# Two attention layers on one core: weight loads traced behind the next block's maxima and tied behind the latest transposes; merges in three steps instead of four

## The chip, the cores and the metric

The kernel runs on 1 core of a Trainium2 chip. The metric is the device time of one execution in microseconds; the time of a kernel is the median of its runs.

## What is computed

A trunk of two layers over x (1 x 1024 x 1024, fp32) with its own weights in each:

```python
for i in range(DEPTH):                       # DEPTH = 2: layer A, layer B
    h = mixer_a(x, ...) if i == 0 else mixer_b(x, ...)
    x = layer_norm(DEEPNORM_ALPHA * x + h, ln_g[i], ln_b[i])
    gate = sigmoid(x @ ple_w_gate[i])
    x = x + gate * (p[i] @ ple_w_proj[i])
```

mixer_a is a windowed attention with 16 heads of 64 in three groups of dilation 1, 4 and 16, each with queries, keys and values of its own, merged by the sums of their softmaxes (x @ w_in is 1024 x 10240). mixer_b is a causal window of 128 with 2 key-value heads for 16 query heads and a sink per head. Either output is multiplied by SiLU(z) and by an output matrix.

## The kernel before

**Arithmetic.** Every fp32 operand of a matmul is split into two fp16 parts, high and low, and a product is three matmuls. A *lin tile* (lines 268 to 270) is 128 tokens by 512 columns: 8 slices x 3 = 24 matmuls of 128x512.

**Weights.** They come in blocks of 1024 x 512 (4 bytes each, 2 MB). `Block.load` (L102) issues four DMAs of 512 KB on SP's queue into the tile `wraw`, of which there are two. `Block.maxima` (L108) lets DVE take the largest absolute value of each chunk, and derives a power-of-two scale. `Block.split` writes the high part on ACT (L131) and the low part on DVE (L132), chunk by chunk, into `whl` (or `wo`, `wg`). `weight_steps` (L554) is a generator that puts these steps in the order split of block i, load of block i + 2 (its `wraw` is then free), maxima of block i + 1; each lin tile pulls 1.6 of its steps (`progress`), `next_block` as many as the block still needs.

**Attention.** A tile of queries and keys goes through `rope_out`: rotation on DVE (L344) and POOL (L346, L347), the parts on ACT (L353) and POOL (L354), a copy on DVE (L357), and a transposing DMA on SP (L358) into `qk` (in layer B `bq`, `bk`). A *score unit* has its matmuls at L381, masked maxima on DVE (L385, L387), exp on ACT (L391), the parts on ACT (L395) and on POOL or DVE (L397), and a transposing DMA (L400) into `pT`. A *value unit* (L412 to L414) multiplies pT with the values; in layer A its result goes through ACT (L655) and SP (L664) to scratch memory `scr`, in layer B through DVE (L815, tile `mu`) and SP (L817) to `ob`. A value unit stands two score units behind its own in layer A, three in layer B.

**Merges.** For each token tile and head pair of layer A a generator `merge` (L697) fetches the three groups (L705), weighs them (L710 to L719) on DVE and ACT, sums on POOL and DVE (L724 to L727) and stores `oa` (L728). `merge_step` takes one step of at most two merges at a time.

**Stages.** Startup; layer A (20 blocks: for each of two pairs of heads and each of three groups a block of values and two of queries and keys, then two blocks of z); `mixed`, which fetches rows of attention output and z (L851, L852, tiles `ot`, `og`), splits them on ACT and DVE (L259, L260), transposes them (L831, `ogT`), multiplies by the output blocks and normalizes; `gate` (x @ ple_w_gate, L933 to L945); layer B (one block of keys and values, two of queries, two of z, whose rows are stored at L686); `mixed` and `gate` again.

**Order.** The program is traced in the order in which Python runs; a planner with a timeline of its own then decides in which order each engine gets its instructions, so that all engines' orders move when the trace does. All DMAs named here go through SP's one queue, in SP's order.

## Time and profile before

| | us |
|---|---|
| median of 3 runs | 1745.78 (1745.37 to 1746.15) |
| profiled execution | 1743.35 |
| its span | 1741.6 |
| PE busy | 1598.4 (92%) |
| DVE, ACT, POOL busy | 1162.5 (67%), 837.5 (48%), 707.3 (41%) |
| mean granted clock of PE | 0.973 |

The table's busy times are sums over the span. Stages lie one behind the other in the profiled execution: startup to some 108 us, layer A to 1091, its projection and gate to some 1300, layer B to 1530, its projection and gate to the end. A number in brackets behind a row of the timeline is the time for which the engine was idle ahead of it, and what ended that.

### The profile page before, as it was taken

The page shows a single profiled execution, that of the slowest core. Times are in us where ns is not written, and L with a number is a line of the kernel's source. Part 1 is how long each engine was busy: PE and PEld are TensorE (multiplying, and loading weights), DVE is VectorE, ACT ScalarE, POOL GpSimd, SP SyncE. Part 2 cuts the span into 40 slices and gives each one's busy share as a digit, 9 for nine tenths or more (in the row PEclk, how much of TensorE's full clock was granted, in tenths as well). Part 3 has the DMA queues.
Part 4 walks back from the last instruction along what each step waited for, and adds up shares of the span by engine and source line. Part 5 has one row for each costly group of instructions (what it writes and reads, how often), then busy time and mean ns, then how long its engine had stood idle before and what let it go on. Part 6 is the DMA issues. An engine that isn't in the chain of part 4 may idle for free. (4 is left out here: it accounts for less than half of the span.)

```text
span 1741.6 us, 29174 instructions
## 1 busy us (share of the span) xinstructions
PE 1598.4 (92%) x10579; PEld 882.9 (51%) x10579; DVE 1162.5 (67%) x2845; ACT 837.5 (48%) x1818; POOL 707.3 (41%) x603
## 2 busy tenths in 40 slices
PE   8599899999999889999999989589999898979998
PEld 3245566664555545666545544234465555534444
DVE  2666665765677677567656776787457988667741
ACT  3422755565455445545546553532334668744221
POOL 0303642551554575335326554343324553123441
PEclk9799999999999999999999999799999999989999
DMA  9325775575688778558647896979974798797973
GB/s 362 149 85 139 141 177 124 129 142 110 153 178 193 186 164 176 131 130 162 140 113 152 162 244 208 315 219 254 261 182 107 145 192 178 146 283 214 236 204 109
DMA packets 542785, 309.06 MB, mean 177 GB/s; under 512 B 473008, under 2 KB 494128, under 8 KB 542256
## 3 DMA queue, kind: packets, MB, share of 16 engines
q1 hardware_dynamic: 542640, 307.20, 71.8%
q8 instruction: 83, 1.36, 0.3%
q14 instruction: 62, 0.51, 0.1%
HBM read 135.82 MB, written 54.92 MB: 110 GB/s over the span
## 5 line engine op out<-in xcount | busy, mean ns | idle before, releaser
L268 PE MATMUL lin<-whl,xhl 128*128 128x512 f16 x1280 | 490.9, 384 | 2.4 <-ACT whl L131 1.9
L269 PE MATMUL lin<-whl,xhl 128*128 128x512 f16 x1280 | 489.2, 382 | 0.0
L270 PE MATMUL lin<-whl,xhl 128*128 128x512 f16 x1280 | 488.9, 382 | 0.0
L391 ACT ACTIVATE sm<-sm,st,cs 128x128 f32<-128x128 f32 (+1 forms) x384 | 203.6, 531 | 167.0 <-DVE st L387 138.7
L397 POOL TENSOR_TENSOR phl<-sm,phl 128x1024 f16<-128x1024 f32 (+1 forms) x88 | 161.3, 1833 | 255.7 <-ACT phl L395 249.9
L108 DVE TENSOR_REDUCE wpm<-wraw 128x1 f32<-128x1024 f32 (+1 forms) x132 | 156.6, 1198 | 94.7 <-DMA wraw<-in_wa_dram 46.9
L270 PEld LDWEIGHTS <-xhl 128*128 128x128 f16 x1280 | 149.4, 117 | 128.9 <-issue 5.1
L268 PEld LDWEIGHTS <-xhl 128*128 128x128 f16 x1280 | 149.5, 117 | 122.7 <-issue 6.7
L269 PEld LDWEIGHTS <-xhl 128*128 128x128 f16 x1280 | 150.3, 117 | 117.5 <-issue 4.3
L346 POOL TENSOR_TENSOR t<-t,t 128x256 f32<-128x256 f32 (+1 forms) x120 | 93.0, 775 | 274.6 <-DVE t L344 202.0
L354 POOL TENSOR_TENSOR hl<-t,hl 128x512 f16<-128x512 f32 (+1 forms) x120 | 141.6, 1180 | 101.9 <-ACT hl L353 101.9
L385 DVE CUSTOM_DVE_ANT_0 sm<-s,tab 128x256 f32<-128x256 f32 (+1 forms) x512 | 157.3, 359 | 30.4 <-PE s L381 26.1
L344 DVE TENSOR_TENSOR t<-lin,tab 128x512 f32<-128x512 f32 (+1 forms) x240 | 147.8, 655 | 30.0 <-PE lin L270 30.0
L132 DVE SCALAR_TENSOR_TENSOR whl<-wraw,s,whl 128x1024 f16<-128x1024 f32 (+1 forms) x116 | 160.3, 1426 | 4.1 <-ACT whl L131 4.1
L353 ACT ACTIVATE hl<-t 128x512 f16<-128x512 f32 (+1 forms) x120 | 72.4, 603 | 174.6 <-POOL t L347 155.4
L131 ACT ACTIVATE whl<-wraw,s 128x1024 f16<-128x1024 f32 (+1 forms) x116 | 122.0, 1123 | 25.1 <-DVE s L208 17.8
L270 PE MATMUL lin<-whl,x2T 128*128 128x512 f16 (+1 forms) x320 | 115.0, 359 | 0.0
L268 PE MATMUL lin<-whl,x2T 128*128 128x512 f16 (+1 forms) x320 | 114.9, 359 | 0.0
L269 PE MATMUL lin<-whl,x2T 128*128 128x512 f16 (+1 forms) x320 | 114.7, 359 | 0.0
L395 ACT ACTIVATE phl<-sm 128x1024 f16<-128x1024 f32 (+1 forms) x128 | 110.7, 865 | 2.2
L412 PEld LDWEIGHTS <-pT 128*128 128x128 f16 x800 | 72.3, 98 | 49.3 <-DMA pT<-phl 47.4
L357 DVE COPY hl<-hl 128x512 f16<-128x512 f16 (+1 forms) x104 | 50.6, 487 | 66.4 <-POOL hl L354 66.3
(186 smaller groups left out, 2942.3 us busy)
## 6 DMA issues: line engine op xcount, KB each, us to landing
wraw<-in_wa_dram SPq DMA_DIRECT2D x56, 512.0 KB, 5.5
scr<-st SPq DMA_DIRECT2D x96, 132.0 KB, 2.5
gt<-scr SPq DMA_DIRECT2D x48, 264.0 KB, 3.4
wraw<-in_wav_dram SPq DMA_DIRECT2D x24, 512.0 KB, 5.7
prh<-pro SPq DMA_DIRECT2D x32, 256.0 KB, 2.7
wraw<-in_wg_dram SPq DMA_DIRECT2D x16, 512.0 KB, 7.1
wraw<-in_wb_dram SPq DMA_DIRECT2D x16, 512.0 KB, 4.8
xg<-y SPq DMA_DIRECT2D x16, 512.0 KB, 3.7
```

What stands on the lines that cost most here:

```text
L108: k.nc.vector.tensor_reduce(pm[:, c:c + 1], self.raw[:, c * q:(c + 1) * q], axis=AX.X, op=ALU.max, apply_absolute_value=True)
L131: nc.scalar.activation(hl[:, 0, sl], self.raw[:, sl], AF.Copy, scale=self.s)
L132: nc.vector.scalar_tensor_tensor(hl[:, 1, sl], self.raw[:, sl], self.s, hl[:, 0, sl], op0=ALU.mult, op1=ALU.subtract)
L268: mm(ps, xh(kt), wh, start=(kt == 0), stop=False)
L269: mm(ps, xh(kt), wl, start=False, stop=False)
L270: mm(ps, xl(kt), wh, start=False, stop=(kt == NK - 1))
L344: nc.vector.tensor_mul(tv, pv, tb[:, n, :].unsqueeze(1).to_broadcast([P, 2 * nh, 32]))
L354: nc.gpsimd.tensor_sub(hl[:, :nh, HD:P], rv, hl[:, :nh, 0:HD])
L385: nc.vector.tensor_tensor_reduce(sm[:, h, :nk], ps[:, i, :nk], mask, 1.0, -3e38, ALU.add, ALU.max, mx[:, h:h + 1])
L391: nc.scalar.activation(sm[:, h, :nk], sm[:, h, :nk], AF.Exp, bias=nbias[:, h:h + 1], scale=cs, accum_out=sums[:, h:h + 1])
L395: nc.scalar.activation(hl[:, 0], sm[:, :, :nk], AF.Copy)
L397: eng.tensor_sub(hl[:, 1], sm[:, :, :nk], hl[:, 0])
```

## The change

`weight_steps` now traces the load of block i + 2 behind the maxima of block i + 1. `rope_out` and `transpose_rows` note the transposing DMA that they traced last (`self.last`), and `Block.load` traces its four DMAs within `issue_after` of that instruction: the planner does not issue them before it. In `merge` one `yield` is gone, so that weights, sum and POOL's multiplications are one step.

```diff
--- before.py
+++ after.py
@@ -94,6 +94,13 @@
         self.done = self.released = False
 
     def load(self):
+        if self.k.last is not None:
+            with self.k.tc.issue_after(self.k.last.ins):
+                self.transfers()
+        else:
+            self.transfers()
+
+    def transfers(self):
         k = self.k
         self.n = NK * self.cols
         self.raw = k.raw.tile([P, NK * 512], F32, tag="wraw", name="wraw")
@@ -152,6 +159,7 @@
         self.o_ps = self.ps_o.tile([P, 2, 4, HD], F32, tag="o", name="o")
         self.o_i = 0
         self.uid = 0
+        self.last = None
         self.bufs = 2
         self.pw = self.wg = None
         self.due = []
@@ -355,7 +363,7 @@
             if nk:
                 src, to = (hl[:, a:b, :].rearrange("p h (w c) -> p h w c", w=2) for a, b in ((nq, nh), (nh, nb)))
                 nc.vector.tensor_copy(to, src[:, :, ::-1, :])
-            nc.sync.dma_start(dst, hl[:, :nb, :].rearrange("p b c -> p (b c)"), transpose=True)
+            self.last = nc.sync.dma_start(dst, hl[:, :nb, :].rearrange("p b c -> p (b c)"), transpose=True)
 
         self.ends.append(parts)
 
@@ -559,10 +567,10 @@
         yield from b[0].maxima()
         for i in range(len(b)):
             yield from b[i].split()
+            if i + 1 < len(b):
+                yield from b[i + 1].maxima()
             if i + 2 < len(b):
                 b[i + 2].load()
-            if i + 1 < len(b):
-                yield from b[i + 1].maxima()
 
     def next_block(self):
         b = self.blocks[self.bi]
@@ -710,7 +718,6 @@
         nc.vector.tensor_reduce(M, nb.rearrange("p g a h -> p a h g"), axis=AX.X, op=ALU.min)
         nc.vector.tensor_sub(w, M.unsqueeze(1).to_broadcast([P, 3, 2, 4]), nb)
         nc.scalar.activation(w, w, AF.Exp)
-        yield
         wl = sp.tile([P, 3, 2, 4], F32, tag="mwl", name="mwl")
         nc.vector.tensor_mul(wl, w, sums)
         L = sp.tile([P, 2, 4], F32, tag="mL", name="mL")
@@ -828,7 +835,7 @@
         self.split(src, s, hl[:, 0, :], hl[:, 1, :])
 
         t = self.tp.tile([P, 2, NK, P], F16, tag="T", name=name)
-        nc.sync.dma_start(t.rearrange("p a k c -> p (a k) c"), hl.rearrange("p a c -> p (a c)"), transpose=True)
+        self.last = nc.sync.dma_start(t.rearrange("p a k c -> p (a k) c"), hl.rearrange("p a c -> p (a c)"), transpose=True)
         dst[i] = t
 
     def mixed(self, l, xres, gate_pool):
```

**How the order moves.** Around the first blocks of layer A's second pair of heads (values, then queries and keys) SP had, before (qk is a transposed query-key tile, pT transposed probabilities, gt, oa and scr belong to merges and value units):

```order
L400 DMA_TRANSPOSE pT<-phl 128x16x128
L705 DMA gt<-scr_0_619 128x528
L705 DMA gt<-scr_0_620 128x528
L728 DMA oa_607<-gt 128x2x256
L664 DMA scr_0_618<-st 128x264
L705 DMA gt<-scr_0_618 128x528
L102 DMA wraw<-in_wa_dram 128x1024 x4
L705 DMA gt<-scr_0_619 128x528
L705 DMA gt<-scr_0_620 128x528
L664 DMA scr_0_618<-st 128x264
L358 DMA_TRANSPOSE qk<-hl 128x12x128
L705 DMA gt<-scr_0_618 128x528
```

and now:

```order
L713 DMA gt<-scr_0_618 128x528
L713 DMA gt<-scr_0_619 128x528
L713 DMA gt<-scr_0_620 128x528
L735 DMA oa_606<-gt 128x2x256
L672 DMA scr_0_618<-st 128x264
L713 DMA gt<-scr_0_619 128x528
L713 DMA gt<-scr_0_618 128x528
L713 DMA gt<-scr_0_620 128x528
L672 DMA scr_0_618<-st 128x264
L366 DMA_TRANSPOSE qk<-hl 128x12x128
L735 DMA oa_607<-gt 128x2x256
L713 DMA gt<-scr_0_618 128x528
```

The four loads of the block have gone from here; in the new order the next loads stand 17 rows further on, behind six more qk and four more pT transposes. In the whole of layer A a block's four loads stand in one piece (before, mostly one and three with transposes between them), on average six lin tiles later in PE's order; at the five later blocks of values the loads of two blocks stand close together, with one qk and one or two pT transposes between them.

On DVE the place is the split of block 7 (s_3692 before, s_3687 now). Before:

```order
L132 SCALAR_TENSOR_TENSOR whl<-wraw,s_3692,whl 128x1024
L387 TENSOR_SCALAR st<-mx,ncs_3195 128x4
L132 SCALAR_TENSOR_TENSOR whl<-wraw,s_3692,whl 128x1024 x3
L357 COPY hl<-hl 128x512
L365 SCALAR_TENSOR_TENSOR vl<-lin,vh 128x2x256
L385 ISA sm,mx<-s,tab 128x128
L385 ISA mx 128x1
L385 ISA sm,mx<-s,tab 128x128
L385 ISA mx 128x1
```

now:

```order
L139 SCALAR_TENSOR_TENSOR whl<-wraw,s_3687,whl 128x1024
L395 TENSOR_SCALAR st<-mx,ncs_3195 128x4
L139 SCALAR_TENSOR_TENSOR whl<-wraw,s_3687,whl 128x1024 x3
L115 TENSOR_REDUCE wpm<-wraw 128x1 x2
L365 COPY hl<-hl 128x512
L115 TENSOR_REDUCE wpm<-wraw 128x1
L373 SCALAR_TENSOR_TENSOR vl<-lin,vh 128x2x256
L393 ISA sm,mx<-s,tab 128x128
L393 ISA mx 128x1
```

The maxima (L108, now L115) that stand behind the split are those of the next block, two at once and a third behind a copy; before, a rotation's copy, a value part and the score maxima (shown as ISA) came first. On PE value units stand later: in layer A ten of the 96 by 0.8 to 1.4 lin tiles, the others less or not; in layer B by 1 tile at the beginning, rising to 3.9 for the last ones. Behind the last value unit of layer B 111 lin matmuls stood before the first one that reads `ogT`; now there are 17.

On SP, ahead of layer B's output projection (t is the row's ot, zb a store of z, y the residual rows), before:

```order
L686 DMA zb_13520<-zu 128x512
L851 DMA ot<-ob_13511 128x1024
L102 DMA wraw<-in_wg_dram 128x1024 x3
L686 DMA zb_13521<-zu 128x512
L102 DMA wraw<-in_wg_dram 128x1024
L852 DMA og<-zb_13519 128x1024
L831 DMA_TRANSPOSE ogT<-rhl 128x16x128 x2
```

now:

```order
L858 DMA ot<-ob_13511 128x1024
L859 DMA og<-zb_13519 128x1024
L838 DMA_TRANSPOSE ogT<-rhl 128x16x128
L873 DMA y<-x_0_12910 128x1024
L858 DMA ot<-ob_13512 128x1024
L838 DMA_TRANSPOSE ogT<-rhl 128x16x128
L109 DMA wraw<-in_wg_dram 128x1024 x4
```

The four loads (`in_wg`) have moved from ahead of the first two ogT transposes to behind them. Ahead of layer A's projection the loads move in the same way, behind the first ogT; the last step of the last merge stands one z tile later in DVE's order.

## Rows read from the trace of the kernel before

**Rows 1.** The page, part 1: busy time of each engine, its share of the span, instructions.

```profile
PE 1598.4 (92%) x10579; PEld 882.9 (51%) x10579; DVE 1162.5 (67%) x2845; ACT 837.5 (48%) x1818; POOL 707.3 (41%) x603
```

**Rows 2.** The waits of PE from 180 to 1090 us (layer A): engine, operation, line, what it waited for; us in total, times, longest.

```profile
PE o L412 <- DMA pT<-phl: 32.3, 22, 3.6
PE s L381 <- DMA qk<-hl: 5.5, 2, 5.2
```

**Rows 3.** PE's timeline, lin matmuls without a stop, the first and the last of 35: start, us, operation.

```profile
604.69 0.38 PE L269 MATMUL lin<-whl,xhl 128*128 128x512 f16 x1
...
612.03 0.38 PE L270 MATMUL lin<-whl,xhl 128*128 128x512 f16 x1
```

**Rows 4.** PE's timeline in layer A, single instructions at the end of a gap; in brackets the idle time before them and what ended it. All are the first matmul of a value unit, except the third, which is that of a score unit. The first two rows are the first and the last of four such stops, the fourth and the fifth the first and the last of ten, the sixth and the seventh the first and the last of three (the prediction says of which kind).

```profile
212.29 0.20 PE L412 MATMUL o<-vh,pT 128*128 128x64 f16 x1 [3.38 <-DMA pT<-phl]
...
1021.65 0.20 PE L412 MATMUL o<-vh,pT 128*128 128x64 f16 x1 [3.57 <-DMA pT<-phl]
...
617.64 0.50 PE L381 MATMUL s<-qk 128*128 128x128 f16 x3 [5.23 <-DMA qk<-hl]
...
351.81 0.20 PE L412 MATMUL o<-vh,pT 128*128 128x64 f16 x1 [0.30 <-DMA pT<-phl]
...
964.87 0.20 PE L412 MATMUL o<-vh,pT 128*128 128x64 f16 x1 [1.46 <-DMA pT<-phl]
...
264.07 0.20 PE L412 MATMUL o<-vh,pT 128*128 128x64 f16 x1 [1.15 <-DMA pT<-phl]
...
725.45 0.20 PE L412 MATMUL o<-vh,pT 128*128 128x64 f16 x1 [0.94 <-DMA pT<-phl]
```

**Rows 5.** SP's timeline around the score unit of the third row of Rows 4: when a DMA was issued, how long the issue took.

```profile
604.79 1.87 SPq L102 DMA_DIRECT2D wraw<-in_wa_dram  x4
...
611.76 1.98 SPq L358 DMA_TRANSPOSE qk<-hl  x1
```

**Rows 6.** The qk tiles, 605 to 620 us: time from issue to landing.

```profile
DMA to landing us min/median/max: 3.7/4.7/5.8
```

**Rows 7.** DVE's timeline, same place.

```profile
609.15 1.22 DVE L108 TENSOR_REDUCE wpm<-wraw 128x1 f32<-128x1024 f32 x1 [0.25 <-DMA wraw<-in_wa_dram]
...
610.98 0.76 DVE L357 COPY hl<-hl 128x512 f16<-128x512 f16 x1
```

**Rows 8.** Windows: stretch, its length, busy time (and instructions) of PE, PEld, DVE, ACT, POOL, the granted clock, the DMA share, GB/s.

```profile
213.00:217.00 4.00, 4.00 (x17) 1.55 (x14) 1.21 (x6) 3.60 (x11) 1.97 (x3) 0.57 1.07 232
616.00:623.00 7.00, 5.36 (x19) 2.50 (x20) 6.39 (x18) 0.74 (x2) 3.90 (x5) 0.51 0.72 169
1022.00:1026.00 4.00, 4.00 (x28) 1.74 (x25) 3.94 (x11) 1.71 (x4) 3.21 (x3) 0.57 0.87 232
```

**Rows 9.** SP's timeline, two transposes of layer A.

```profile
206.05 3.00 SPq L400 DMA_TRANSPOSE pT<-phl  x1
...
1014.42 5.18 SPq L400 DMA_TRANSPOSE pT<-phl  x1
```

**Rows 10.** The waits of SP's queue in layer A (180 to 1090 us).

```profile
SPq L400 <- POOL hl L354: 71.9, 22, 5.5
SPq L400 <- POOL phl L397: 70.0, 19, 6.2
```

**Rows 11.** The waits of DVE in layer A (180 to 1090 us).

```profile
DVE wpm L108 <- DMA wraw<-in_wa_dram: 42.8, 19, 6.2
...
DVE mwl L715 <- ACT mw L712: 5.0, 8, 2.6
```

**Rows 12.** Line 132 on DVE (the low part of the split), 330 to 470 us: count, min/median/max ns, first and last start, forms.

```profile
L132 DVE SCALAR_TENSOR_TENSOR whl<-wraw,s,whl x12: 1271/1278/2180, 335.9 to 434.7; 128x1024 f16<-128x1024 f32 x12
```

**Rows 13.** PE's timeline, the first matmul of layer A's output projection.

```profile
1112.31 0.58 PE L268 MATMUL lin<-whl,ogT 128*128 128x512 f16 x1 [20.94 <-DVE whl L132]
```

**Rows 14.** SP's timeline ahead of layer A's output projection.

```profile
1094.77 0.90 SPq L102 DMA_DIRECT2D wraw<-in_wg_dram  x2
...
1105.09 4.95 SPq L831 DMA_TRANSPOSE ogT<-rhl  x1
```

**Rows 15.** The last value unit of layer B on PE (count, ns, first and last start).

```profile
L412 PE MATMUL o<-bvh,pT x8: 193/193/202, 1529.3 to 1529.9; 128*128 128x64 f16 x8
```

**Rows 16.** DVE's timeline behind the last value unit of layer B.

```profile
1533.73 1.22 DVE L108 TENSOR_REDUCE wpm<-wraw 128x1 f32<-128x1024 f32 x1 [5.95 <-DMA wraw<-in_wg_dram]
```

**Rows 17.** SP's timeline ahead of layer B's output projection.

```profile
1552.28 1.34 SPq L102 DMA_DIRECT2D wraw<-in_wg_dram  x3
...
1557.93 6.09 SPq L831 DMA_TRANSPOSE ogT<-rhl  x1
```

**Rows 18.** PE's timeline, the first matmul of layer B's output projection.

```profile
1566.09 0.61 PE L268 MATMUL lin<-whl,ogT 128*128 128x512 f16 x1 [12.04 <-DMA ogT<-rhl]
```

**Rows 19.** The waits of PE from 1300 to 1530 us (layer B).

```profile
PE o L412 <- DVE mu L815: 17.7, 10, 3.9
PE o L412 <- DMA pT<-phl: 4.1, 4, 1.7
PE s L381 <- DMA bq<-hl: 1.5, 1, 1.5
```

**Rows 20.** Line 102 (loads), the stretch and the columns of Rows 12.

```profile
L102 SPq DMA_DIRECT2D wraw<-in_wa_dram x8: 327/423/433, 342.3 to 437.6; - x8
```

**Rows 21.** The waits of PE over the whole program: the one for weights once the blocks run.

```profile
PE lin L268 <- ACT whl L131: 1.9, 1, 1.9
```

## The prediction

> **What bounds the kernel now.** I read the page first: PE is busy for 1598.4 us of the 1741.6 us span [rows 1], so no other engine bounds the whole, and what a change of order can win is PE's stops. The waits of PE, asked for stage by stage, tell who ends them. In layer A (180 to 1090 us) value units wait 32.3 us in 22 stops for the transposed probabilities pT, and score units 5.5 us for qk [rows 2]. The lin tiles around them run without a stop, 34 steps in 7.34 us, so 0.216 us a matmul and 5.2 us a tile of 24 [rows 3]. A value unit that stood one tile later in PE's order, or whose transpose landed a few us sooner, would not stop.
>
> The timeline of SP tells why they land late. I sort the stops by what SP issued ahead of the transpose. The score unit (5.23 us) and **four** value units (the largest stops with a load, 10.9 us together) follow chunks of a weight load by a few us; **ten** small ones (10.1 us together) have a load a little further ahead; **three** (4.5 us together) lie at a block of values, where there are no qk transposes [rows 4]. The remaining five pT stops (6.8 us) have no load near. The rows of the score unit show that a load delays twice. On SP, four chunks were issued from 604.79, the qk transpose at 611.76, and its issue alone took 1.98 us [rows 5]; it landed after 5.8 us where the quickest of that stretch took 3.7 [rows 6]. On DVE a maximum ran at 609.15, as soon as its chunk was there, ahead of the copy at 610.98 that the transpose needed [rows 7]. After such stops the granted clock falls to the 1.2 GHz level: 0.57 over 213 to 217, 0.51 over 616 to 623, 0.57 over 1022 to 1026 [rows 8]; the four us at 0.57 lose 1.7, the 5.36 busy us at 0.51 lose 2.6. Two pT transposes at the first and the last of these places needed 3.00 and 5.18 us for the issue alone [rows 9].
>
> Against this reading stands SP's own list of waits: it holds transposes back mostly for POOL's subtractions, 71.9 and 70.0 us for the two largest entries [rows 10]. Many transposes are late because vector engines are.
>
> **The change, part by part.** The sum is made against the profiled execution, 1743.35 us, which lies 2.43 us under the median of 1745.78.
>
> *Loads behind the maxima and tied.* Bytes, maxima and splits stay the same in number. In the new order a block's four chunks stand together on SP, behind a transpose, some six lin tiles later than before. DVE loses waits for chunks (42.8 us in layer A for the largest source [rows 11]). I cost that at nothing by itself: it is idle time of an engine off the path, covered by PE's lin tiles, and if that cover were gone it would show as a late pT. What is queued behind the moved maxima matters more: DVE now does the split and up to four maxima in a row, 4 x 1.28 + 4 x 1.22 = 10 us [rows 7, 12], and behind them stand the copies of L357 and the score maxima of L385, on which ACT's exp, POOL's subtraction and SP's transposes wait. Value units stand about a tile (0.8 to 1.4) later in PE's order at these places, which pays for half of the 10 us; the maxima, 4.9 of it, stood near there before too.
>
> Layer A, stop by stop:
> - The score unit: no load stands around its transpose any more. The maximum's 1.22, the 2.1 of late landing (5.8 less 3.7) and half of the lost clock (1.3) go: **-4.5**. Bounds 0 and -7.8 (stop and clock).
> - The four: at the first, the 6.2 us from issue (206.05 [rows 9]) to the unit's start (212.29) shrink to 3.7, so 2.5 of its 3.38 go. The same share of 10.9 is 8; of the two clock dips of 1.7 I count 2.5: **-10.5**. Bounds -3 and -14.3.
> - The ten: the loads leave some and come to stand ahead of others; half, **-5**. Bounds 0 and -10.
> - The three at blocks of values: two blocks, eight chunks, now stand a few rows apart there. **0**; bounds -4.5 and +4 (one more stop like the first of the four).
> - The five without a load: **0**; bounds -4 and +4, inside their own 6.8.
>
> Together -20.
>
> *Layer A to its projection.* PE stops for 20.94 us, until 1112.31 [rows 13], at the end of a chain whose last link is the ogT transpose: issued at 1105.09, 4.95 us in its issue, behind chunks issued from 1094.77 on [rows 14]. The new order has the first ogT ahead of these chunks. With the quickest landing, 3.7 us, PE would start 3.5 us sooner; the last step of the last merge stands a z tile's work later on DVE, for which I take 1.5 off: **-2**. Bounds -5 and +4.
>
> *Layer B to its projection.* Here the change takes cover away. Between the last value unit (1529.3 [rows 15]) and the first matmul that reads ogT stood 111 lin matmuls, now 17: 94 x 0.216 = 20.3 us less. Against that the chain from the unit to ogT gets shorter. A maximum that waited 5.95 us for its chunk ahead of the unit's normalization [rows 16] is gone from there. The transpose issued at 1557.93, 6.09 us in its issue behind chunks of 1552.28 [rows 17], let PE start at 1566.09 [rows 18]; now it stands ahead of the chunks, and with 3.7 us to landing PE starts 4.4 us sooner. Net 20.3 - 5.95 - 4.4 = +10. What it buys: value units stand 1 to 3.9 tiles later in PE's order, so 5 to 20 us more slack for the 23.3 us of stops inside layer B [rows 19] and one clock dip of 1.7. I take half of these 25, -12.5, since 17.7 us of the stops end at DVE's normalization, which an order of PE doesn't quicken: **-2.5**. Bounds +10 (nothing regained) and -15.
>
> *Merges in three steps.* The instructions are the same; a merge ends one step earlier. DVE's multiplication now follows ACT's exp in one step: it waited 5.0 us in 8 places before [rows 11], so at most some 5 us more idle time on DVE, under lin tiles. **0**; bounds -1 and +2.
>
> Sum: -20 - 2 - 2.5 = -24.5, so 1718.85 profiled and **1721.3** as a median.
>
> **The rivals.**
> 1. *The loads only move.* A load behind one transpose stands ahead of the next. For it: eight chunks at blocks of values. Against it: most large stops lie where the new order has no load. Only -4.5 of the score unit and -2.5 of the four stay, the rest is 0: -7, a median of 1738.8. Chance 0.14.
> 2. *Layer B's cover is not regained.* For it: DVE ends most stops there. -20 - 2 + 10 = -12: 1733.8. Chance 0.10.
> 3. *Both.* -7 - 2 + 10 = +1: 1746.8, no change. Chance 0.12.
> 4. *Slower: the vector engines set the transposes.* The place is the 10 us of split and maxima on DVE with the score maxima behind them. For it: SP's waits for POOL [rows 10]. A queue that is free earlier wins only 3 us in A, and the end of layer B still costs 10: +7, a median of 1752.8. It decides where A, B and the passage between them regain less than 10 us together. Chance 0.13.
> 5. *Slower: weights come late.* Blocks were loaded from 342.3 on and split some 90 us later, until 434.7 [rows 12, 20]; loaded at about 385, some 46 us are left, where landing (5.8), maxima (4.9) and the scale take under 20. Before, one stop on weights is known, 1.9 us [rows 21]. If each of 20 later blocks gave one, 38 us would stand against the forecast's gain: 1759.3. Chance 0.03.
>
> The Trainium skill ("DMA: Bandwidth & Descriptors", section "Rules for kernel authors") says to issue a DMA early and to wait for its semaphore late; this change does the reverse, and by that rule the fifth rival would be the likeliest. No run here shows the rule's cost yet: the trace has 46 us to spare.
>
> **How the numbers follow.** The forecast's own chance is 0.48. Rivals 1 and 2 are faster too: 0.48 + 0.14 + 0.10 = 0.72. Within 0.2% (3.5 us, about what a measurement of this kernel can tell from no change) is rival 3, 0.12. Slower: 0.13 + 0.03 = 0.16. The low end goes half of the way from each term to its lower bound, -30, -3.5 and -9: 1703. The high end, 1750, takes in rivals 1 to 3. Left out are rivals 4 and 5 (0.16) and some 0.04 below.
>
> **What would show it.** Right: no stop over 2 us where the score unit stopped, and full clock there; 10 to 18 us of pT stops in layer A where there were 32.3; DVE's waits for chunks there under 15 us; mu stops in layer B near 9 us; some 22 us of stop ahead of layer B's projection. Wrong: pT stops in A of 25 us or more with SP held by POOL as before (rival 4), large stops at blocks of values (rival 1), layer B's stops as they were (rival 2), lin tiles that wait for whl (rival 5).

## The result: 1.2% slower, and the profile after

The changed kernel takes 1764.05 us (median of 4 runs, 1761.18 to 1772.46), the kernel before 1745.57 (4 runs, 1742.90 to 1746.15): ratio 1.0117, 95% interval 1.0081 to 1.0153. The forecast was 1721.3 (1703 to 1750), so sign and range are wrong. The profiled execution took 1761.18 us (span 1759.4). Part 1 of its page answers to [rows 1]:

```profile
PE 1599.0 (91%) x10579; PEld 883.5 (50%) x10579; DVE 1158.3 (66%) x2845; ACT 836.1 (48%) x1818; POOL 705.6 (40%) x603
```

PE is busy for as long as before, to 0.6 us. So nearly all of the 17.8 us by which the span grew are stops, and the question is where. Lin matmuls come in the same sequence in both traces; the start of the same one, after minus before, makes a ledger. Its differences from mark to mark are what a stage lost (+) or won (-). The last two columns give the same figure for the runs below, from one profiled execution of each: those that load the blocks of the stage as before (5 or 6 runs), and those that load them as the change does (7 to 9); a run whose own edit touches the stage in another way is left out.

| stage | until (us, before) | forecast | measured | shift at its end | other runs, as before | other runs, as changed |
|---|---|---|---|---|---|---|
| startup | 114.7 | 0 | -1.2 | -1.2 | | |
| layer A | 1069.9 | -20 | -2.0 | -3.2 | -0.8 to +5.7 | -3.5 to +5.6 |
| A to its projection | 1135.4 | -2 | +6.5 | +3.3 | -2.4 to +0.7 | +4.7 to +6.5 |
| A's projection, gate | 1290.3 | 0 | +2.6 | +5.9 | -1.5 to +1.4 | +2.9 to +7.4 |
| B, and to its projection | 1589.2 | -2.5 | +2.5 | +8.4 | -4.5 to -0.7 | +3.7 to +7.9 |
| B's projection, gate | 1734.2 | 0 | +9.4 | +17.8 | 0.0 to +4.1 | -0.5 to +9.5 |

A few us of one execution say little: the first run below is as quick as before, yet its kept execution (1752.27 us, the slowest of its ten) moves between -1.4 and +5.6 within layer A. Read so, layer A won little if anything. The way from A to its projection, A's projection, and B with the way to its projection cost time in every run that has the change there. In the last stage the two ranges overlap. Waits of PE from 180 to 1090 us, as [rows 2]:

```profile
PE o L420 <- DMA pT<-phl: 29.7, 20, 3.9
PE s L389 <- DMA qk<-hl: 7.4, 1, 7.4
```

pT's stops fell by 2.6 us, where 14 to 22 were forecast, and the score unit's stop grew from 5.23. The same value units, one by one, in both traces (us of stops for pT, in the prediction's groups):

| value units | before | forecast | now |
|---|---|---|---|
| the four | 10.9 | -8 | 5.0 |
| the ten | 10.1 | -5 | 1.7 |
| the three at blocks of values | 4.5 | 0 | 6.9 |
| the five without a load | 6.8 | 0 | 4.3 |
| eight that did not stop for pT before | | no term | 11.9 |

The stops that were to go did go, and others came. Say that a transpose has a load in flight when one of the four chunks was issued ahead of it and has not landed when it is issued. By the issue and landing times of the traces that was so for 25 of the 96 pT transposes of layer A before (5.50 us to landing on average, the others 3.92) and for 14 now (6.45, the others 4.00). The stops behind those with a load in flight fell from 24.1 to 14.7 us; the stops behind the others rose from 8.2 to 15.0. The clock gave nothing either: PE runs at the 1.2 GHz level in four stretches of layer A, as before (now 548 to 551, 610 to 620, 1005 to 1009 and 1036 to 1039 us, at 0.50 each; before, those of [rows 8] and 551 to 555).

PE's timeline, the places of [rows 4] (first row of the four, the score unit) and, between them, a block of values:

```profile
216.92 0.20 PE L420 MATMUL o<-vh,pT 128*128 128x64 f16 x1 [1.47 <-DMA pT<-phl]
...
268.99 0.20 PE L420 MATMUL o<-vh,pT 128*128 128x64 f16 x1 [2.44 <-DMA pT<-phl]
...
614.10 0.50 PE L389 MATMUL s<-qk 128*128 128x128 f16 x3 [7.38 <-DMA qk<-hl]
```

At the first the stop shrank from 3.38 to 1.47, and the granted clock of 213 to 217 is 1.00 where it was 0.57 [rows 8]. It still stops, because the load of a block now stands here. SP's timeline:

```profile
203.97 2.28 SPq L109 DMA_DIRECT2D wraw<-in_wa_dram  x4
206.36 7.11 SPq L408 DMA_TRANSPOSE pT<-phl  x1
```

Tied behind one transpose, the four chunks stand directly ahead of the next. Its issue took 7.11 us where it took 3.00 [rows 9]. At the value block another took 7.79, behind seven chunks of two blocks, and the stop grew from 1.15 to 2.44.

At the score unit no load is near. SP issued the transpose late, and it landed 3.8 us later, as quick as any:

```profile
610.25 1.43 SPq L366 DMA_TRANSPOSE qk<-hl  x1
```

POOL and then DVE show why (timelines):

```profile
602.89 1.04 POOL L729 TENSOR_TENSOR gt<-gt,mw 128x512 f32<-128x512 f32 x1 [0.79 <-DVE mw L726]
603.90 1.04 POOL L730 TENSOR_TENSOR gt<-gt,mw 128x512 f32<-128x512 f32 x1
604.90 1.60 POOL L362 TENSOR_TENSOR hl<-t,hl 128x512 f16<-128x512 f32 x1
```

```profile
606.83 0.93 DVE L722 TENSOR_TENSOR mwl<-mw,gt 128x24 f32<-128x24 f32 x1 [0.29 <-ACT mw L720]
607.80 0.18 DVE L724 TENSOR_REDUCE mL<-mwl 128x8 f32<-128x24 f32 x1
607.90 1.28 DVE L352 TENSOR_TENSOR t<-lin,tab 128x512 f32<-128x512 f32 x2
609.09 0.19 DVE L725 RECIPROCAL mL<-mL 128x8 f32<-128x8 f32 x1
609.32 0.70 DVE L726 TENSOR_TENSOR mw<-mw,mL 128x24 f32<-128x24 f32 x1
609.94 0.28 DVE L365 COPY hl<-hl 128x512 f16<-128x512 f16 x1
```

Steps of a merge (L722 to L730) stand ahead of the subtraction of L362 and of the copy of L365 that the transpose reads.

**A to its projection.** PE's first matmul there, as [rows 13]; then ACT and DVE ahead of it:

```profile
1115.48 0.58 PE L276 MATMUL lin<-whl,ogT 128*128 128x512 f16 x1 [27.32 <-DVE rhl L268]
```

```profile
1101.67 4.25 ACT L138 ACTIVATE whl<-wraw,s 128x1024 f16<-128x1024 f32 x4
...
1105.83 1.13 ACT L267 ACTIVATE rhl<-og,rs 128x1024 f16<-128x1024 f32 x1
```

```profile
1102.84 6.90 DVE L139 SCALAR_TENSOR_TENSOR whl<-wraw,s,whl 128x1024 f16<-128x1024 f32 x4
1109.66 1.27 DVE L268 SCALAR_TENSOR_TENSOR rhl<-og,rs,rhl 128x1024 f16<-128x1024 f32 x1
```

The split of the first gate block now stands ahead of the split of the first row: 4.2 us on ACT, 6.8 on DVE. Before, the row went first:

```profile
1102.22 1.15 ACT L259 ACTIVATE rhl<-og,rs 128x1024 f16<-128x1024 f32 x1 [0.80 <-DVE rs L208]
...
1103.47 1.59 DVE L260 SCALAR_TENSOR_TENSOR rhl<-og,rs,rhl 128x1024 f16<-128x1024 f32 x1 [0.61 <-issue]
```

PE's release by name, "DVE rhl", ended at 1110.93; what it waited for was the transpose behind it, issued at 1110.96.

**A's projection.** A new stop, at a small matmul for the scale of the keys/values block (SP, DVE, PE):

```profile
1168.10 2.24 SPq L109 DMA_DIRECT2D wraw<-in_wbkv_dram  x4
```

```profile
1172.47 0.69 DVE L115 TENSOR_REDUCE wpm<-wraw 128x1 f32<-128x512 f32 x1 [0.77 <-DMA wraw<-in_wbkv_dram]
```

```profile
1183.36 0.26 PE L241 MATMUL s<-mdd,ones 128*128 128x128 bf16 x1 [8.61 <-DVE ri L215]
```

A block is late for PE although no lin matmul waits for its weights: the scale stands in PE's order ahead of the next rows' tiles. (What the matmul reads is `mdd`, which DVE finished at 1183.32.) The late load is one part of it. The last maximum ended at 1176.26, and the four small steps from there to `mdd` took DVE another 7.1 us, because splits and sums of rows stand between them.

**B and its projection.** PE's waits from 1300 to 1545 us, as [rows 19]; the last value unit, as [rows 15] (its time last); the first projection matmul, as [rows 18]:

```profile
PE o L420 <- DVE mu L822: 12.1, 6, 4.3
PE s L389 <- DVE mx L393: 3.6, 2, 2.9
```

```profile
L420 PE MATMUL o<-bvh,pT x8: 192/193/193, 1549.4 to 1550.0; 128*128 128x64 f16 x8
```

```profile
1575.92 0.61 PE L276 MATMUL lin<-whl,ogT 128*128 128x512 f16 x1 [22.17 <-DMA ogT<-rhl]
```

From the last unit to this matmul it takes 26.5 us where it took 36.8, yet the stop grew from 12.04 to 22.17, since the lin tiles that covered it have gone ahead.

**Last projection.** One late row, before and now, then SP's wait of 1626 to 1646 us and the window 1640 to 1656 (columns of [rows 8]):

```profile
1632.49 0.39 PE L268 MATMUL lin<-whl,ogT 128*128 128x512 f16 x1 [1.20 <-DMA ogT<-rhl]
```

```profile
1648.55 0.61 PE L276 MATMUL lin<-whl,ogT 128*128 128x512 f16 x1 [7.27 <-DMA ogT<-rhl]
```

```profile
SPq L873 <- ACT ot L864: 7.3, 1, 7.3
```

```profile
1640.00:1656.00 16.00, 8.73 (x29) 3.27 (x28) 13.47 (x23) 4.64 (x5) 4.72 (x4) 0.68 1.04 256
```

With the stop came the lower level of the clock: 8.73 busy us at 0.68 lose 2.8. Stop (6.1 more than the 1.20 at the same matmul before) and clock make up 8.9 of the +9.4.

### The profile page after: what moved, and what is told of

The parts are those of the page before. It is cut to its first block, busy times and chain, and to the rows that moved or that the text cites. A ratio compares the mean times of both kernels' runs of the same rounds, so it can differ in the third digit from the quotient of the medians.

```text
span 1759.4 us, 29156 instructions
## 1 busy us (share of the span) xinstructions
PE 1599.0 (91%) x10579; PEld 883.5 (50%) x10579; DVE 1158.3 (66%) x2845; ACT 836.1 (48%) x1818; POOL 705.6 (40%) x603
## 4 chain that ended last, share of the span: by engine, by line
PE 42%; DVE 17%; issue 11%; DMA 11%; POOL 10%; ACT 6%; SPq 2%; POOLq 0%; DVEq 0%; ACTq 0%
PE lin L276 12%; PE lin L278 12%; PE lin L277 12%; DVE wpm L115 3%; POOL hl L362 2%; ACT sm L399 2%; DVE whl L139 2%; POOL phl L405 2%; DMA pT<-phl 2%; DMA gt<-scr 2%; DVE sm L393 2%; PE s L389 1%; POOL t L354 1%; PE lin L489 1%; DVE t L352 1%
## 5 line engine op out<-in xcount | busy, mean ns | idle before, releaser
L362 POOL TENSOR_TENSOR hl<-t,hl 128x512 f16<-128x512 f32 (+1 forms) x120 | 146.5, 1220 | 115.2 <-ACT hl L361 115.2
L115 DVE TENSOR_REDUCE wpm<-wraw 128x1 f32<-128x1024 f32 (+1 forms) x132 | 155.4, 1193 | 55.8 <-DMA wraw<-in_wa_dram 17.4
L139 DVE SCALAR_TENSOR_TENSOR whl<-wraw,s,whl 128x1024 f16<-128x1024 f32 (+1 forms) x116 | 167.3, 1484 | 4.1 <-ACT whl L138 4.0
L365 DVE COPY hl<-hl 128x512 f16<-128x512 f16 (+1 forms) x104 | 49.0, 471 | 96.0 <-POOL hl L362 95.7
L276 PE MATMUL lin<-whl,ogT 128*128 128x512 f16 x128 | 52.1, 407 | 56.8 <-DMA ogT<-rhl 29.4
```

What stands on the lines that cost most here:

```text
L115: k.nc.vector.tensor_reduce(pm[:, c:c + 1], self.raw[:, c * q:(c + 1) * q], axis=AX.X, op=ALU.max, apply_absolute_value=True)
L139: nc.vector.scalar_tensor_tensor(hl[:, 1, sl], self.raw[:, sl], self.s, hl[:, 0, sl], op0=ALU.mult, op1=ALU.subtract)
L276: mm(ps, xh(kt), wh, start=(kt == 0), stop=False)
L362: nc.gpsimd.tensor_sub(hl[:, :nh, HD:P], rv, hl[:, :nh, 0:HD])
```

## The experiments

Ratios are to the kernel before, run on the same chip, with the 95% interval. "Shift" is the ledger's number, from one execution.

### Which edit

Each edit of the change alone, then load and tie together:

```diff
# merges only (e1_merge): only the yield is gone
# maxima only (e2_swap): untied, merges in four steps
+            if i + 1 < len(b):
+                yield from b[i + 1].maxima()
             if i + 2 < len(b):
                 b[i + 2].load()
-            if i + 1 < len(b):
-                yield from b[i + 1].maxima()
# tie only (e3_tie): load() as in the change, ahead of the maxima
# both (e4_swap_tie): the change with the yield back
```

> Only the merge in three steps; loads as before. Theory (the time is lost where a layer passes into its projection, and in the projections, because swap and tie together reorder those stages): as before, 1745 within 4 us, since PE's order in layer B and behind it is the one of before. Rival (the shorter merge puts DVE and POOL work ahead of the copies that qk transposes wait for, as at the 7.4 us score stop near 607 of the changed kernel): most of the 18 us, 1755 or more.

1746.52 us, 1.0017 [0.9998, 1.0037]: no difference shown.

> Only the load traced behind the next block's maxima, not tied, merges in four steps. Theory (swap and tie together reorder the passages): as before, 1745 within 4 us; PE's order in layer B is that of before. Rival (late tracing alone makes weights and maxima late): 1755 or more, with larger waits of DVE for chunks.

1745.37, 1.0017 [0.9999, 1.0034]: none either.

> Only the tie behind the latest transpose, loads traced at the old place, merges in four steps. Theory (both together are needed): between 1740 and 1752, since layer B's value units stand only 0.2 tiles later on average and the cover behind the last one is 4.3 tiles where the changed kernel has 0.7. Rival (the tie alone costs the time): 1758 or more, with a stop near 22 us ahead of layer B's projection.

1749.16, 1.0039 [1.0023, 1.0055]. The tie by itself costs 17.0 us of layer A (shift at its end). PE's waits of 180 to 1100 us:

```profile
PE o L420 <- DMA pT<-phl: 46.0, 28, 4.9
PE s L389 <- DMA qk<-hl: 4.3, 2, 4.1
```

Some 9 us came back later, in B and the passages. 23 of the 96 pT transposes have a load in flight and take 7.30 us to landing, where 25 took 5.50 before.

> Swap and tie, merges in four steps. Theory (merges play no part): 1758 to 1768, as the changed kernel, with the stops of some 22 us ahead of layer B's projection and of 27 us ahead of layer A's. Rival (the merges cost the time): 1750 or less.

1759.94, 1.0104 [1.0072, 1.0135]; shift -3.6 at A's end, +11.0 in A's projection (1185.3), +15.0 behind B. Load and tie together make the loss; the merges add nothing that the intervals can tell. The score unit stops for 8.0 us here, with four steps, so its longer stop does not come from the missing `yield` either.

### Which blocks

Blocks 0 to 19 are layer A's, 20 and 21 its projection's, 22 and 23 the gate's, 24 B's keys/values, 25 to 30 B's others, 31 and 32 the last gate's. In the first three runs only the blocks named are loaded as in the change, with merges in four steps; in the last two all but those named.

```diff
+            late = i + 2 <= 19      # p_le19; 22 to 24: p_22_24; 25 to 30: p_25_30; not 20 to 24: q_not20_24; not 25 to 30: q_not25_30
+            if i + 2 < len(b) and not late:
+                b[i + 2].transfers()
             if i + 1 < len(b):
                 yield from b[i + 1].maxima()
-            if i + 2 < len(b):
+            if i + 2 < len(b) and late:
                 b[i + 2].load()
```

> Swap and tie for the blocks of layer A alone, merges in four steps. Theory (each stage answers to the order of its own loads): layer A gains 2 to 4 us up to its last lin tile, as in the changed kernel, and everything behind it stays as before: 1738 to 1746. Rival (the projection stages pay for what layer A does): a stop ahead of A's projection of 26 us or more, 1750 or more.

1745.04, 1.0011 [0.9989, 1.0032]: no difference shown for layer A's twenty blocks, on which -20 was forecast.

> Swap and tie for the blocks loaded during layer B alone (queries, z, its output blocks). Theory: the stops inside layer B fall by 10 to 12 us, and the passage to its projection costs 13 to 18 us, since the last value unit stands 3.9 tiles later and the cover behind it is 0.7 tile: net 2 to 7 us, 1745 to 1752. Rival (the cover is paid back in full by B): 1743 or less.

1750.52, 1.0046 [1.0027, 1.0066]. Shift -10.5 within B and +20.9 from its end to its projection, +10.4 net: the cover that the prediction saw go, and not enough regained. The stop there, 25.55 us, ends at a block's scale (`PE s L241 <- DVE mdd L234`) and not at the row, so cover is not the whole of it in this run.

> Swap and tie for three blocks alone, those loaded while layer A passes into its projection and gate (two gate blocks, the block of keys and values). Theory: the stop ahead of A's projection grows by some 6 us to 27, and a stop for a block's scale (the small matmul on mdd) appears in the projection, 2 to 8 us: 1750 to 1758. Rival (these blocks don't matter): 1745 within 3 us.

1746.69, 1.0014 [0.9994, 1.0034], below the 1750 to 1758 expected. The stop at the scale came (9.18 us). The one ahead of A's projection did not grow (18.59; 27 expected): these three blocks alone do not make it.

> The changed kernel with the old order and no tie for the five blocks 20 to 24 (layer A's output blocks, its gate blocks, the block of keys and values). Theory (their late loads cost the passage to A's projection and the stop for a block's scale inside it): the stop ahead of A's projection is back at 21 us, the stop of 8.6 us for the scale of the keys-and-values block is gone, together 8 to 12 us: 1752 to 1756. Rival (these stops come from merges and rows): 1760 or more.

1757.16, 1.0087 [1.0060, 1.0113]. A's passage stops for 22.59 us, the scale stop is gone; the time is a little above what was expected.

> The changed kernel with the old order and no tie for blocks 25 to 30, those loaded during layer B. Theory (B's order loses more cover behind the last value unit than its stops give back): value units of B stand as before, the stop ahead of B's projection is back near 12 us, and the kernel gains 3 to 10 us: 1754 to 1761. Rival (B as changed is a gain): 1765 or more.

1749.23, 1.0034 [1.0012, 1.0055]. The largest part, some 15 us less than the change, and quicker than expected (1754 to 1761). PE ahead of B's projection:

```profile
1570.34 0.61 PE L276 MATMUL lin<-whl,ogT 128*128 128x512 f16 x1 [7.43 <-DMA ogT<-rhl]
```

The parts do not add: B's blocks cost some 8 us put late alone, and some 15 when everything else is late already.

### What holds the transposes in layer A

```diff
# x_noload: the kernel before without the loads of blocks 2 to 19
+        if 2 <= i <= 19:
+            self.raw = k.blocks[i % 2].raw
+            return
# x_nomax: the change, maxima of these blocks over 1/16 of a chunk
+            w = q // 16 if 2 <= k.blocks.index(self) <= 19 else q
# x_nomerge: the change, merges of the first pair without arithmetic
+        if pair == 0:
+            yield
+            nc.sync.dma_start(...)   # gt, group 0, stored as it is
+            return
# m_before, m_after: no merge steps traced around the score stop
+        if self.hold:
+            return
```

> The kernel before without the weight loads of blocks 2 to 19: they take their raw weights from the tiles of blocks 0 and 1 (values of layer A are thus of other weights); every maximum and split stays. Theory (in layer A most stops come from the vector engines' order, not from loads in SP's queue): value units still wait 15 us or more for pT in layer A, the score stop near 610 stays above 4 us, the gain is under 20 us. Rival (the recorded one: loads in the queue make transposes late): pT stops in layer A under 10 us, the score stop under 2, a gain of 30 us or more.

1740.86, 0.9987 [0.9969, 1.0005]. PE's waits in layer A:

```profile
PE o L416 <- DMA pT<-phl: 15.8, 11, 2.8
PE s L385 <- DMA qk<-hl: 6.0, 3, 4.2
```

No difference is shown in the time. Without any load half of pT's stops stay, and the score unit still stops for 4.23 us. The sum over A's 96 pT transposes from issue to landing is 388.4 us; before 415.5, with the change 418.3, with the tie alone 461.3. All of the loads delay them by 27 us, and the change left that as it was. The 96 qk transposes are another matter: 392.0 without loads, 427.6 before, 407.3 with the change, 404.5 with the tie alone. In layer A `self.last` is always a qk transpose, so the tie clears the way of these, and PE seldom waits for them. (The run lost 13.3 us between 130 and 150 us, where lin tiles waited for splits, and won 14.1 from 180 us to A's end, so with no load at all some 14 us of layer A were there to win, by this one execution.)

> The changed kernel with the maxima of blocks 2 to 19 taken over a sixteenth of each chunk (a block's scale is thus that of fewer weights): DVE's burst of maxima behind a split is 0.4 us instead of 4.9. Theory (in layer A the vector engines' order sets the transposes, the burst being part of it): pT stops in layer A fall from 30 to 20 us or less, the score stop near 607 stays, 10 to 15 us less than the changed kernel. Rival (the queue sets them): 1760 or more.

1754.99, 1.0066 [1.0044, 1.0089]; pT's stops 31.4 us. One unit has 8.05 of them, at 1031 us, where it had 3.87; the others fell from 25.8 to 23.4. So the burst of maxima on DVE (rival 4) sets little of them. The score stop fell to 5.04, and the shift at A's end is -7.4 against -3.2. The time lies between what theory (10 to 15 us less than the change) and rival (1760 or more) expected.

> The kernel before with no merge step taken from the fifth tile of the second pair's first block of values until the third tile of its first block of queries and keys (the steps come later); loads as before, with the four chunks at their place. Theory (the score stop near 612 is the chain of the block's first qk tile, held up by merge steps on POOL and DVE): the stop falls from 5.2 to under 3 us, the half clock behind it may go, 1736 to 1743. Rival (the recorded one, the four chunks ahead of the transpose): the stop stays at 5 us, 1745.

> The changed kernel with the same pause of the merge steps. Theory: the score stop near 607 falls from 7.4 to under 4 us, with 4 to 7 us less than the changed kernel, 1757 to 1761. Rival: the stop stays above 6 us.

1745.71, 1.0015 [0.9995, 1.0034], and 1764.47, 1.0124 [1.0092, 1.0155]; score stops 5.05 and 7.44. The merge's instructions stayed where they were on DVE and POOL, so these two tell nothing.

> The changed kernel with the merges of the first pair of heads left out but for their loads and their store (that half of layer A's output is one group's alone): no merge step on DVE, ACT and POOL around 607. Theory (the first qk tile behind a block of values waits for merge steps on DVE and POOL): the score stop falls from 7.4 to under 4 us, stops of value units between 560 and 600 get smaller, 1757 to 1761. Rival (the chain of that tile is longer than the two lin tiles that cover it, whatever else the engines do): the stop stays above 5 us.

1749.17, 1.0038 [1.0017, 1.0058], quicker than the 1757 to 1761 expected. PE's waits in A, where no qk is left:

```profile
PE o L420 <- DMA pT<-phl: 21.3, 16, 3.1
PE o L420 <- ACT st L663: 6.6, 3, 5.0
PE o L420 <- ACT vh L372: 1.2, 1, 1.2
```

The merges hold the qk transpose of that place; that is shown. Without them A gains 10.6 us over the change (shift -13.8 against -3.2).

### The passages

```diff
# x_tiesplit: the change, the split of block 22 traced behind that of the first row
+                if k.blocks.index(self) == 22:
+                    for i in k.row:
+                        es.enter_context(k.tc.issue_after(i.ins))
# x_y5: the change, the sixth row's residual load behind the seventh ogT
+                with self.tc.issue_after(self.og[6].ins):
+                    nc.sync.dma_start(y, xres(n))
# x_xg3: x_y5, and the fourth row's store too
+                with self.tc.issue_after(self.og[6].ins):
+                    nc.sync.dma_start(xg_dr[n], y)
# x_fix3: x_tiesplit and x_xg3, and block 24 loaded as before
+            late = i + 2 != 24
```

> The changed kernel with one more tie: the split of the first gate block (whl) stays behind the split of the first row of attention output on ACT and DVE; nothing else in those two orders moves there. Theory (the longer stop ahead of layer A's projection comes from that split, 4.25 us on ACT and 6.9 us on DVE ahead of the row): PE's first matmul on ogT starts 4 to 7 us sooner, the stop is 20 to 23 us instead of 27.3, 1755 to 1761. Rival (the late loads or the transpose's landing set it): the stop stays above 25 us, 1762 or more.

1756.53, 1.0090 [1.0059, 1.0121]. The stop fell to what was expected, and the passage lost 0.9 us where the change lost 6.5. In the whole time the interval overlaps that of the change (1.0081 to 1.0153), so the gain is shown at this place only:

```profile
1109.39 0.59 PE L281 MATMUL lin<-whl,ogT 128*128 128x512 f16 x1 [22.14 <-ACT ot L871]
```

> The changed kernel with one load moved: that of the sixth residual row of the last projection stays behind the transpose of the seventh row of attention output. Theory (SP stands for 7.3 us with that load, until a row tile comes free, with a transpose behind it that PE needs): the stop of 7.3 us near 1641 is gone and the last stages cost 6 to 9 us less: 1754 to 1760. Rival (the transpose is late for its own row's sake): the stop stays above 5 us, 1762 or more.

1763.86, 1.0123 [1.0089, 1.0156]; the stop is 6.57 us. SP is held at the next thing in its order:

```profile
SPq L898 <- POOL y L897: 9.8, 2, 7.9
```

> The changed kernel with two DMAs of the last projection moved behind the transpose of the seventh row of attention output: the sixth residual load and the store of the fourth normalized row, on which SP stood for 7.9 us when the load alone was moved. Theory (SP is held by whichever of them is issued ahead of that transpose): the stop near 1641 falls from 7.3 to under 2 us, 6 to 9 us less than the changed kernel: 1754 to 1760. Rival (the row itself is late): the stop stays above 5 us, 1762 or more.

1764.57, 1.0118 [1.0093, 1.0143]; 6.72 us, SP held 8.1 us at the store of the row before that. With both DMAs moved SP stands at a third, so these two runs alone don't acquit it. The changed kernel's trace does; DVE, the low part of the seventh row:

```profile
1641.25 1.27 DVE L268 SCALAR_TENSOR_TENSOR rhl<-og,rs,rhl 128x1024 f16<-128x1024 f32 x1
```

It ended at 1642.52. SP was free from 1640.59; it issued another row's transpose (1641.39, 2.59 us) and this one's at 1644.08. SP delays the row by 1.6 us at most: the row itself is late, and that theory falls. What makes it late stays open.

> The changed kernel with three edits at once: the first gate block's split behind the first row's, the keys-and-values block loaded in the old order and untied, and the two DMAs of the last projection moved. Theory (the time over the kernel before is three stops of the projections, each of its own): the stop ahead of A's projection 22 us, no stop for the keys-and-values block's scale, none over 2 us near 1641, together 14 to 20 us less than the changed kernel: 1744 to 1750, no faster than the kernel before. Rival (what is removed at one stop returns at the next): 1755 or more.

1758.85, 1.0080 [1.0052, 1.0109]; 1744 to 1750 was expected. The passage keeps 21.7 us, the scale stop is gone, but the rows behind it stop now, and 6.9 us are lost there from 1185.3 to 1226.9. PE's waits of 1085 to 1300 us:

```profile
PE lin L281 <- ACT ot L877: 21.7, 1, 21.7
PE lin L281 <- DMA ogT<-rhl: 5.0, 4, 3.4
PE lin L281 <- DVE y L898: 3.7, 3, 2.9
PE lin L281 <- DVE p2t L211: 2.0, 1, 2.0
```

Some of a stop that is taken away comes back at the next. No version beat the kernel before.

## Why the prediction was wrong, point by point

- **Layer A, -20 (measured -2.0): the step that failed most.** Not the terms that were to shrink: the four and the ten lost 14.3 us of stops, where 13 were forecast. What failed are the terms at 0 beside them. "No load stands around its transpose any more" was read from the places that had stopped. Eight other units stop now, for 11.9 us, and the three at blocks of values grew by 2.4. Part of it is the first rival (0.14): a load tied behind one transpose stands ahead of the next. Fewer pT transposes have a load in flight (14 for 25), but each takes longer (6.45 us for 5.50), and the sum from issue to landing stays (415.5 and 418.3 us). The larger part is not: only 2.8 of the 11.9 us lie at transposes with a load in flight, the stops without one rose from 8.2 to 15.0, and with no load at all 15.8 us of stops stay. So some 16 us of the 32.3 were never the loads' to give. What sets the new ones stays open; two of the eight (183 and 194 us, 3.2 us together) stand 0.7 and 1.2 lin tiles earlier in PE's order than before. At the rows at 203.97 and 206.36 the chunks landed from 209.8 to 213.7 us and the transpose issued behind them at 216.9. The Trainium skill ("DMA: Bandwidth & Descriptors", section "Two DMAs through the same engine are not ordered") says that within one queue of one DMA engine descriptors start in order, and these landings agree.
- **Score unit, -4.5.** The load ahead of it was real but not the last cause: without loads 4.23 of 5.23 us stay. In the changed kernel merge steps on POOL and DVE are: the stop goes without merges. Neither "no stop over 2 us" nor "full clock" came true (7.38 us, and 0.50 over 610 to 618).
- **A to its projection, -2 (measured +6.5).** The ogT transpose got ahead of chunks as forecast; the split of a gate block got ahead of the row it needs. The prediction followed SP there and gave ACT and DVE only 1.5 us for a last merge step. Tying that split back won 5.6 us of it.
- **A's projection, 0 (+2.6).** Late blocks were looked for as lin matmuls that wait for weights (rival 5); there are none in A, where DVE's waits for chunks fell to 14.4 us as forecast (under 15). But block 24 stops PE for 8.61 us at its scale. Rival 5 holds at this one block: taking blocks 20 to 24 back removes the stop, while layer A's 20 blocks, loaded as late, show no cost. The Trainium skill ("DMA: Bandwidth & Descriptors", section "Rules for kernel authors") says to issue a DMA early; this case agrees at that one block.
- **B and its passage, -2.5 (+2.5).** The stop ahead of the projection was right (22.17, "some 22"), and so was +10: the chain got 10.3 us shorter and the stop 10.1 longer. What failed is the size of what it buys: B's stops fell from 23.3 to 16.7, so 6.6 for the 12.5 forecast. The clock gave nothing there: 0.79 over 1500 to 1508 before, 0.83 over 1380 to 1390 and again over 1482 to 1492 now. The mu stops are 12.1, not 9. This is rival 2, and taking B's blocks back won the most. The +2.5 is the least of all executions with this order (+3.7 to +7.9 in the others).
- **Merges, 0.** Right.
- **Last projection, 0 (+9.4).** No step spoke of it. The row that PE waits for until 1648.55 us and the clock are where it goes, and SP is not the cause; what makes the row late stays open. Part of it is not the change's: with the order of before the stage moves between 0.0 and +4.1 from run to run, with that of the change between -0.5 and +9.5, so the kept execution of the kernel before was a quick one there.
- **Rival 4, slower.** The sign is its own, the place isn't: maxima of a sixteenth left the pT stops at 31.4 us. Vector engines do set stops elsewhere, by merge steps ahead of a qk tile, a split ahead of a row and row steps ahead of a scale. Its point of decision held: A, B and the passage between them regained less than the 10 us.

Open too: which blocks turn the order in A's passage (22 to 24 alone don't, all but 20 to 24 don't; no run had 20 to 24 alone), and what holds the 15.8 us of pT stops that stay without loads.

## What to carry to other kernels

A load that is moved in a queue still stands ahead of something: price it at its new place with the same row that priced the old one, and look for the ceiling, the time without the load at all. A stop that goes at one unit can come back at another that had none, so a list of the units that stop today is not the whole sum. Where a planner orders several engines from one trace, moving work early or late changes the order on all of them; look at the passages between layers engine by engine, for a split, a scale or a row's step that has come to stand ahead of the one that PE needs next. Cover that an edit takes from the end of a stage is a sure cost; slack that it gives inside the stage is a hope, and here half of it came.

## What was not expected of the hardware

The issue of one transposing DMA took from 1.43 us (610.25, nothing ahead) to 7.11 us behind four chunks and 7.79 behind seven: SP itself is held that long, and with it whatever is next in its order. Chunks are not the only thing that does this: at 1115.35 us an issue took 5.70, with another transpose and small rows ahead and no chunk. Taking all loads away quickens the mean pT transpose only from 4.33 to 4.05 us (415.5 and 388.4 over 96), because before only 25 of the 96 had a load in flight. The granted clock was 1.00 around a PE stop of 1.47 us where a stop of 3.38 had 0.57 before [rows 8]. Two stops of nearly the same length differ: after one of 2.44 us (269 us) the clock stayed at 1.00, after one of 2.35 (1004.8 us) it was 0.50 over 1005.5 to 1008.8. Around the stop of 7.27 us the mean of 16 us was 0.68, so partly at the level of 1.2 GHz.
